# Long convolution of a hybrid layer: folding the forward transform by token parity, adding the bias to the spectrum by DMA, and moving its first half among the hyena projections

## The chip, the cores and the metric

The kernel runs on one core of one Trainium2 chip. The metric is the device time of one execution in microseconds (us), as the median of several executions. TensorE (PE) does the matrix products, VectorE (DVE) and ScalarE (ACT) the elementwise work, GpSimd (POOL) and SyncE (SP) mostly issue DMA transfers.

## What is computed

One layer of a diffusion backbone on 256 latent tokens and 256 context tokens, width 2048, all in float32. A half-step feed-forward block (SwiGLU) comes first and last. Between them one projection feeds two groups of heads: grouped-query attention, and a hyena mixer of width 1024 on the latent tokens. The change is in the mixer:

```
def long_conv(v, kk):                      # v: 256 tokens x 1024 channels, kk: 512 taps
    vf = rfft(v, n=2 * L); kf = rfft(kk, n=2 * L)
    return irfft(vf * kf, n=2 * L)[:L]

def hyena_mixer(u, kk, conv_w, conv_b, hy_bias):
    uc = short_conv(u, conv_w, conv_b)     # three taps
    x0, x1, v = split(uc)
    v = v * x1
    v = long_conv(v, kk) + hy_bias * v
    return v * x0
```

The transform of 256 tokens to 257 frequencies is done as matrix products with cosines and sines, and so is the way back. A term `hy_bias * v` is the same as adding the bias to every value of the real spectrum of the filter.

## The kernel before

**Precision.** Every float32 operand of a product is split in two parts, high and low, in a reduced type that PE takes at full rate: ACT casts the high part, DVE subtracts it from the original to get the low part (`split`, lines 216 to 220; `weight`, lines 237 to 251, for weights that come by DMA as `raw`). `mm3` (lines 253 to 256) then makes three products of each pair: high by high, high by low, low by high (lines 254, 255, 256).

**Order.** The program is written straight down. A planner gives each engine a fixed order when the program is built: among the instructions that its own cost estimates say are ready, the one that stands first in the program. So work of later lines fills gaps when its inputs and its buffers are there. A buffer pool has a fixed number of slots: weights have four `raw` slots, three `whi` and three `wlo` slots; PSUM has four banks `pa` and four `pb`. The DMA transfers of a queue (SP's or POOL's) are issued in that queue's own order.

**Stages around the change**, in the order of time:

1. End of the first feed-forward block's down projection (`Ffn.down`, lines 628 to 659). Its main passes use products of 512 columns; its last two groups (`rest`) are done once for the context tokens and once for the latent tokens, with products of 256 columns, 24 of them for each weight piece of 512 KB (`raw<-in_w_dn`). Between the two kinds stand, in program order, the loads of constants for the mixing stage (`mload`, lines 1068 to 1084): two transform matrices `dftc` and `dfts`, tables for attention and the short convolution, the bias `hyb`, and sixteen loads of the filter's spectrum from DRAM scratch into four tiles `kspec` of 128 frequencies x 1024 channels (real parts in `kspec[0]`, `kspec[1]`, imaginary ones in `kspec[2]`, `kspec[3]`; line 1084, each load 128 rows of 256 channels). All go through SP's queue. The spectrum itself was computed much earlier, beside the first block (`filter_spectrum`); row 0 of its imaginary part carries the 257th frequency.
2. The norms and the key and value projections.
3. The hyena projections: a loop over eight channel tiles `ct` (lines 1232 to 1241). Each takes four weight pieces (`proj_pair`, lines 1219 to 1229: 16 steps of one 512-column and one 256-column product for each of two outputs), then the short convolution `conv` on ACT and DVE (lines 1208 to 1217), which gives the tile `vT[ct]`, and a transpose of a piece of the residual (`turn_x`).
4. The long convolution (lines 1244 to 1294), two halves of 512 channels. A half transposes four `vT` tiles to token-major (lines 1257 to 1262), splits them, multiplies by the cosine and sine matrices (for each of two blocks of 128 frequencies two banks, two token blocks, three products: 12 products of 512 columns a block, 24 a half), multiplies by the filter's spectrum on DVE (lines 1272 to 1281, with three one-row corrections for the packed row 0), splits the result, multiplies back (48 products of 256 columns a half, lines 1286 to 1292) and adds bias times `vT` on DVE while it leaves PSUM (line 1293). Between the blocks the loop advances the first query projection by `QSTEP` weight pieces, so that PE has other work while DVE is busy.
5. The second query projection, the gate projections `x0`, attention (lines 1297 to 1359) and the output projection.

Of the kernel before, what the change touches and what calls it, by code (L numbers as in the profile page):

```python
# [15 lines left out]
ALU = mybir.AluOpType  # L16
# [27 lines left out]

AWAKE = (17, 5)

QSTEP = (2, 1, 3, 2)
FILL = (2, 0)

AWAKE2 = 8  # L50
# [19 lines left out]
def hybrid_layer_kernel(ctx: ExitStack, tc: tile.TileContext, a):  # L70
# [14 lines left out]
    def U(shape, dt=F32):  # L85
        return T(up, shape, "u", dt, 58)

    def tmp(shape):
        return T(up, shape, "sq", bufs=2)
# [7 lines left out]
    def PB(shape=(P, 512)):  # L97
        return T(pp, shape, "pb")
# [117 lines left out]
    def split(src, shape):  # L216
        hi, lo = U(shape, F32R), U(shape, F32R)
        S.copy(hi, src)
        V.tensor_sub(lo, src, hi.bitcast(F32))
        return hi, lo  # L220
# [847 lines left out]
    def mload(name, shape, src=None):  # L1068
        t = T(mp, shape, name)
        nc.sync.dma_start(t, a[name] if src is None else src)  # L1070
        return t

    dftc = mload("dftc", (P, 2, L))
    dfts = mload("dfts", (P, 2, L))
    rope = mload("rope", (P, 2, 2, 64))
    qkg = mload("qkg", (P, 2, P), a["qkg"].partition_broadcast(P))
    convw = mload("convw", (P, 3, 3 * CT))
    convb = mload("convb", (P, 3 * CT))
    hyb = mload("hyb", (P, CT))
    gout = mload("gout", (P, 2 * CT))  # L1080
    kspec = [T(mp, (P, HW), f"kspec{s}") for s in range(4)]
    for n, t in enumerate(spec):
        for f in range(2):
            nc.sync.dma_start(kspec[2 * (n % 2) + f][:, (n // 2) * L : (n // 2 + 1) * L], t[:, f, :])

    f1.hook = lambda: None
    next(more)
# [141 lines left out]
                yield  # L1229

    vT = [U((P, 2, L)) for _ in range(CT // 2)]
    for ct in range(CT):
        pvx = []
        for _ in proj_pair(a["w_hy"][ct], pvx):
            pass
        yv = conv(pvx[0], 2 * CT + ct)
        y1 = conv(pvx[1], CT + ct)
        V.tensor_mul(vT[ct // 2][:, ct % 2, :], yv, y1)
        turn_x(ct % 2, ct // 2)
        if ct == 4:  # L1240
            turn_gates()


    hyT = [U((P, 2, L)) for _ in range(CT // 2)]
    fwd = [split(m, (P, 2, L)) for m in (dftc, dfts)]
    inv = []
    for name in ("idfc", "idfs"):
        m = tmp((P, 2, L))
        nc.sync.dma_start(m, a[name])
        inv.append(split(m, (P, 2, L)))  # L1250
    pq0 = []
    query = proj_steps(a["w_q"][0], [0, 1], pq0)
    next(query)
    for half in range(2):
        hs = slice(half * 512, half * 512 + 512)
        vt = []
        for t in range(2):
            pt = PB((P, 4, P))
            for i in range(4):
                ct = half * 4 + i  # L1260
                PE.transpose(pt[:, i, :], vT[ct // 2][:, ct % 2, t * P : (t + 1) * P], ident)
            vt.append(split(pt.rearrange("p a b -> p (a b)"), (P, 512)))
        yre, yim = [], []
        for f in range(2):
            pr_, pi_ = PB(), PB()
            for ps, mat in ((pr_, fwd[0]), (pi_, fwd[1])):
                for t in range(2):
                    mm3(ps, [m[:, t, f * P : (f + 1) * P] for m in mat], vt[t], t == 0, t == 1)
            kr, ki = kspec[f][:, hs], kspec[2 + f][:, hs]
            a1, a2 = U((P, 512)), U((P, 512))  # L1270
            b1, b2 = U((P, 512)), U((P, 512))
            V.tensor_mul(a1, pr_, kr)
            V.tensor_mul(a2, pi_, ki)
            V.tensor_mul(b1, pr_, ki)
            V.tensor_mul(b2, pi_, kr)
            if f == 0:
                V.tensor_copy(b2[0:1, :], a2[0:1, :])
                V.memset(a2[0:1, :], 0.0)
                V.memset(b1[0:1, :], 0.0)
            V.tensor_sub(a1, a1, a2)  # L1280
            V.tensor_add(b1, b1, b2)
            yre.append(split(a1, (P, 512)))
            yim.append(split(b1, (P, 512)))
            for _ in range(QSTEP[2 * half + f]):
                next(query, None)
        for i in range(4):
            ct = half * 4 + i
            ps = PB((P, L))
            sl = slice(i * P, (i + 1) * P)
            for n, (y_, mat) in enumerate(((yre, inv[0]), (yim, inv[1]))):  # L1290
                for f in range(2):
                    mm3(ps, [m[:, sl] for m in y_[f]], [m[:, f, :] for m in mat], n + f == 0, n + f == 2)
            V.scalar_tensor_tensor(hyT[ct // 2][:, ct % 2, :], vT[ct // 2][:, ct % 2, :], hyb[:, ct : ct + 1], ps,
                                   op0=ALU.mult, op1=ALU.add)


    def gate_steps():
# [541 lines left out]
def _constants():  # L1839
    f32 = np.float32  # L1840
    rows = L // 64
    row = np.repeat(np.arange(rows), 64).astype(f32)
    col = np.tile(np.arange(64), rows).astype(f32)
    inv = (f32(10000.0) ** (-np.arange(0, 64, 2, dtype=f32) / f32(64))).astype(f32)
    ang = np.concatenate([row[:, None] * inv, col[:, None] * inv], axis=-1).astype(f32)
    rope = np.stack([np.cos(ang.astype(np.float64)), np.sin(ang.astype(np.float64))], axis=1).astype(f32)
    rope = rope.reshape(2, P, 2, 64).transpose(1, 0, 2, 3)

    t = np.linspace(0.0, 1.0, L, dtype=f32)[:, None]
    w = (f32(2.0 * math.pi) * np.arange(L, dtype=f32)[:, None] / f32(L)).astype(f32)  # L1850
    f = np.linspace(1e-4, 15, 16, dtype=f32)[None, :]
    fw = (f * w).astype(f32).astype(np.float64)
    z = np.concatenate([t, np.cos(fw).astype(f32), -np.sin(fw).astype(f32)], axis=-1).astype(f32)

    eo = np.r_[0:L:2, 1:L:2]
    z = z[eo]
    tneg = np.stack([*(-t[:, 0])[eo].reshape(2, P), 1.0 - 2.0 * (np.arange(P) % 2)], axis=1).astype(f32)

    n = np.arange(L)
    th = 2.0 * np.pi * np.outer(n, n) / (2 * L)  # L1860
    alt = (1.0 - 2.0 * (n % 2))
    cos_, sin_ = np.cos(th), np.sin(th)

    fdft = np.stack([m[eo, :P].reshape(2, P, P) for m in (cos_, sin_)])
    fdft[1, 1, :, 0] = 1.0 - 2.0 * (np.arange(P) % 2)
    fdft = fdft.transpose(2, 0, 1, 3).astype(f32)

    fr = np.r_[0 : P + 1, L - 1 : P : -1]

    def tp(m):  # L1870
        return np.ascontiguousarray(m.reshape(2, P, -1).transpose(1, 0, 2)).astype(f32)

    sinv = sin_.copy()
    sinv[:, 0] = alt
    wt = np.full((L, 1), 2.0)
    wt[0] = 1.0
    ic = cos_ * wt / (2 * L)
    isn = sin_ * 2.0 / (2 * L)
    isn[0] = alt / (2 * L)
    return dict(rope=np.ascontiguousarray(rope), zT=np.ascontiguousarray(z.T), tneg=tneg,  # L1880
                fdft=np.ascontiguousarray(fdft), dftc=tp(cos_[:, fr]), dfts=tp(sinv[:, fr]), idfc=tp(ic[fr]), idfs=tp(isn[fr]))


def _prepare(i):
# [51 lines left out]
    d["qkg"] = np.stack([eo(i["q_norm"][0]), eo(i["k_norm"][0])])  # L1936
    d["convw"] = c_(i["conv_w"][0].reshape(3, 3 * CT, P).transpose(2, 0, 1))
    d["convb"] = pcol(i["conv_b"][0])
    d["hyb"] = pcol(i["hy_bias"][0])
    d["gout"] = pcol(i["g_out"][0])  # L1940
    w1, w2, w3, d["flt_w4"] = (c_(i[f"flt_w{n}"][0]) for n in (1, 2, 3, 4))
    head = np.zeros((P, 4, 64), np.float32)
# [24 lines left out]
```

## Time and profile before

| | |
|---|---|
| median of three timed executions | 2575.5 us (2574.84 to 2576.6) |
| the profiled execution's own time | 2573.66 us |
| its span | 2571.9 us, 38718 instructions |
| mean granted PE clock | 0.998 |
| busy share PE / DVE / ACT / POOL | 99% / 84% / 47% / 14% |
| hyena projections and long convolution | about 1531 to 1677 us of the span |
| loads of the mixing constants | 1422.7 to 1434.5 us of the span |

A line of the timeline has the start in us from the span's start, the duration, engine, line of the program, operation, output<-inputs, shape, and how many are merged into it; in brackets the idle time before it and what ended that. `PEld` is a weight load, `SPq` a DMA issue of SP. A line of the windows has the stretch, its length, then the busy time and the number of instructions of each engine, the granted clock, the mean busy share of the 16 DMA engines, and GB/s.

### The profile page before, as it was taken

How to read it: one execution, taken by the hardware profiler on the slowest of the kernel's cores; microseconds unless marked ns; L12 is line 12 of the kernel's file. 1: busy time of each engine (PE TensorE's matmuls, PEld its weight loads, DVE VectorE, ACT ScalarE, POOL GpSimd, SP SyncE). 2: the span in 40 equal slices, each digit the busy share in tenths (PEclk: the TensorE clock that was granted, in tenths of full speed). 3: DMA queues.
4: the chain of work that ended last, by engine and by line, in shares of the span. 5: the costliest groups of instructions: out<-in, count | busy, mean ns of one | idle time of the engine just before them, and what ended most of it. 6: DMA issues, size and time to landing. Idle time of an engine off the chain costs nothing.

```text
span 2571.9 us, 38718 instructions
## 1 busy us (share of the span) xinstructions
PE 2555.1 (99%) x14333; PEld 2198.3 (85%) x14333; DVE 2164.1 (84%) x3498; ACT 1213.6 (47%) x1702; POOL 365.1 (14%) x587
## 2 busy tenths in 40 slices
PE   8999999999999999999999999999999999999999
PEld 5678999999999999888888988888888888888887
DVE  6876888888888896777989796789789999999998
ACT  5454444444444443111211455457466666665554
POOL 1132222222222223320010000000000001012010
PEclk9999999999999999999999999999999999999999
DMA  9997889888888899996798556335757878789784
GB/s 364 383 290 209 250 243 254 242 243 248 253 247 255 243 252 317 395 363 209 260 328 287 178 167 194 123 123 162 232 172 237 246 240 265 236 265 310 236 286 159
DMA packets 209387, 640.77 MB, mean 249 GB/s; under 512 B 24715, under 2 KB 27756, under 8 KB 204844
## 3 DMA queue, kind: packets, MB, share of 16 engines
q1 hardware_dynamic: 134396, 482.37, 55.6%
q0 software_dynamic: 74608, 155.78, 23.4%
q8 instruction: 112, 1.84, 0.3%
q14 instruction: 79, 0.65, 0.1%
q10 hardware_dynamic: 192, 0.13, 0.0%
HBM read 558.73 MB, written 48.53 MB: 236 GB/s over the span
## 4 chain that ended last, share of the span: by engine, by line
PE 97%; DMA 1%; DVE 1%; ACT 0%; issue 0%; SPq 0%; ACTq 0%; DVEq 0%
PE pb L254 10%; PE pb L255 10%; PE pb L256 10%; PE pa L254 9%; PE pa L255 9%; PE pa L256 9%; PE pa L1394 6%; PE pa L1395 6%; PE pa L1396 6%; PE pb L1394 4%; PE pb L1396 4%; PE pb L1395 4%; PE pa L262 3%; PE pa L264 2%; PE pa L1110 1%; PE pa L1111 1%
## 5 line engine op out<-in xcount | busy, mean ns | idle before, releaser
L243 ACT CAST whi<-raw 128x1024 fp32r<-128x1024 f32 x235 | 247.2, 1052 | 500.4 <-PE pb L255 192.3
L247 DVE TENSOR_TENSOR wlo<-raw,whi 128x1024 fp32r<-128x1024 f32 x235 | 286.9, 1221 | 134.5 <-ACT whi L243 133.5
L254 PE MATMUL pa<-u,whi 128*128 128x256 f32 (+1 forms) x912 | 306.6, 337 | 2.1 <-ACT u L907 2.1
L255 PE MATMUL pa<-u,whi 128*128 128x256 f32 (+1 forms) x912 | 304.8, 334 | 0.9 <-DVE u L912 0.9
L256 PE MATMUL pa<-u,wlo 128*128 128x256 f32 (+1 forms) x912 | 304.5, 334 | 0.0
L254 PE MATMUL pb<-u,whi 128*128 128x256 f32 (+1 forms) x904 | 300.1, 332 | 0.0
L255 PE MATMUL pb<-u,whi 128*128 128x256 f32 (+1 forms) x904 | 298.4, 330 | 0.0
L256 PE MATMUL pb<-u,wlo 128*128 128x256 f32 (+1 forms) x904 | 298.3, 330 | 0.0
L466 ACT CAST bhi<-raw 128x768 fp32r<-128x768 f32 x111 | 92.5, 833 | 265.1 <-PE pb L255 131.1
L158 DVE CUSTOM_DVE_ANT_0 adas<-adaw,crow,cond 128x1024 bf16<-128x1024 f32 x160 | 205.0, 1281 | 14.5 <-DMA adaw<-in_w_adaT_dram 12.7
L158 DVE CUSTOM_DVE_ANT_0 adas<-adaw,crow,mod 128x1024 bf16<-128x1024 f32 x160 | 205.0, 1281 | 13.3 <-DMA adaw<-in_w_adaT_dram 11.3
L254 PEld LDWEIGHTS pa<-u,whi 128*128 128x128 f32 x912 | 172.9, 190 | 24.6 <-issue 4.5
L255 PEld LDWEIGHTS pa<-u,whi 128*128 128x128 f32 x912 | 173.5, 190 | 17.7 <-DVE u L912 1.7
L256 PEld LDWEIGHTS pa<-u,wlo 128*128 128x128 f32 x912 | 173.5, 190 | 17.2
L254 PEld LDWEIGHTS pb<-u,whi 128*128 128x128 f32 x904 | 171.8, 190 | 17.4 <-issue 2.0
L469 DVE TENSOR_TENSOR blo<-raw,bhi 128x768 fp32r<-128x768 f32 x111 | 106.3, 957 | 94.1 <-ACT bhi L466 94.1
L255 PEld LDWEIGHTS pb<-u,whi 128*128 128x128 f32 x904 | 171.9, 190 | 15.7 <-issue 0.4
L256 PEld LDWEIGHTS pb<-u,wlo 128*128 128x128 f32 x904 | 171.8, 190 | 15.6
L1396 PE MATMUL pa<-whi,u 128*128 128x512 f32 x451 | 175.8, 390 | 0.0
L1394 PE MATMUL pa<-whi,u 128*128 128x512 f32 x450 | 175.7, 391 | 0.0
L1395 PE MATMUL pa<-wlo,u 128*128 128x512 f32 x450 | 175.6, 390 | 0.1
L277 ACT CAST whi<-raw 128x1024 fp32r<-128x1024 f32 x122 | 126.9, 1052 | 98.4 <-DVE raw L277 63.0
(476 smaller groups left out, 6689.8 us busy)
## 6 DMA issues: line engine op xcount, KB each, us to landing
adaw<-in_w_adaT_dram SPq DMA_DIRECT2D x224, 512.0 KB, 5.8
raw<-in_w_up1q_dram SPq DMA_DIRECT2D x124, 512.0 KB, 5.2
raw<-in_w_up2p_dram SPq DMA_DIRECT2D x107, 512.0 KB, 4.7
raw<-in_w_dn_dram SPq DMA_DIRECT2D x94, 512.0 KB, 6.0
u<-act POOLq DMA_DIRECT2D x172, 256.0 KB, 9.6
wrow<-in_w_ada_dram SPq DMA_DIRECT2D x32, 1024.0 KB, 10.1
raw<-in_w_dn2p_dram SPq DMA_DIRECT2D x59, 512.0 KB, 5.3
vraw<-in_w_up2p_dram SPq DMA_DIRECT2D x53, 512.0 KB, 4.8
```

The costliest lines, as they stand in the source:

```text
L158: V.tensor_tensor_reduce(out=sc, in0=t, in1=crow[i][:, b * (D // 2) : (b + 1) * (D // 2)], scale=1.0, scalar=mcol if b else bada[:, c * KT ...
L243: last_hi[0] = S.copy(hi, raw)
L247: last_lo[0] = V.tensor_sub(lo, raw, hi.bitcast(F32))
L254: PE.matmul(ps, w[0], xx[0], start=start, stop=False)
L255: PE.matmul(ps, w[0], xx[1], start=False, stop=False)
L256: return PE.matmul(ps, w[1], xx[0], start=False, stop=stop)
L277: return do(*args, **kw)
L466: return raw, hi, lo, S.copy(hi, raw[:, :, 0:3])
L469: return V.tensor_sub(lo, raw[:, :, 0:3], hi.bitcast(F32))
L1394: PE.matmul(ps[t], hi, w[0], start=start, stop=False)
L1395: PE.matmul(ps[t], hi, w[1], start=False, stop=False)
L1396: last = PE.matmul(ps[t], lo, w[0], start=False, stop=stop)
```

## The change

- **Matrices.** `dftc` and `dfts` (256 tokens x 256 frequencies each) give way to one tile `dftf` of four 128 x 128 blocks: cosine and sine, for even and for odd tokens, at the first 128 frequencies. It is split at `ct == 2` of the hyena loop; the matrices of the way back are loaded and split at `ct == 4` and `ct == 5`.
- **Forward transform.** The transposes now take every second token (`t::2`). For cosine and for sine, one bank gets the product with the even tokens, another that with the odd ones: 12 products of 512 columns for a half instead of 24. ACT copies the odd bank to SBUF; DVE's sum of even and odd gives one block of frequencies, their difference the other, mirrored block. Three one-row copies on ACT repair the packed row.
- **Spectrum product.** The four products per block read SBUF instead of PSUM. The three one-row corrections on DVE are gone; instead row 0 of `kspec[2]` is set to zero, and after the first product with it ACT overwrites row 0 of `kspec[0]` with the row `last_row`.
- **Bias.** The product with `hyb` is gone; PSUM is copied out by ACT. Instead `kspec[0]` and `kspec[1]` get the bias added by two accumulating DMAs of POOL's queue (128 rows of 1024 values, the bias row repeated), and `last_row` by two small ones.
- **Loads.** SP's burst loses `dftc`, `dfts` and `hyb` and gains `dftf`, and four loads of one row each into `last_row`. Of the sixteen `kspec` loads, the four that fill `kspec[2]` leave row 0 out: `r0` is 1 there, so they have rows 1 to 127.
- **Order.** `long_steps(half)` is a generator with seven yields. Half 0 is advanced at each of the three yields of `proj_pair` from `ct == 4` on; half 1 runs after the loop, with `QSTEP` query pieces after each of its yields.

```diff
-QSTEP = (2, 1, 3, 2)
+QSTEP = (1, 1, 1, 1, 2, 1, 1)
...
-    dftc = mload("dftc", (P, 2, L))
-    dfts = mload("dfts", (P, 2, L))
+    dftf = mload("dftf", (P, 4, P))
...
-    hyb = mload("hyb", (P, CT))
...
     for n, t in enumerate(spec):
         for f in range(2):
-            nc.sync.dma_start(kspec[2 * (n % 2) + f][:, (n // 2) * L : (n // 2 + 1) * L], t[:, f, :])
+            r0 = (n % 2) * (1 - f)
+            nc.sync.dma_start(kspec[2 * (n % 2) + f][r0:P, (n // 2) * L : (n // 2 + 1) * L], t[r0:P, f, :])
+    last_row = U((P, 512))
+    for n in range(4):
+        nc.sync.dma_start(last_row[32 * (n // 2) : 32 * (n // 2) + 1, (n % 2) * L : (n % 2 + 1) * L], spec[2 * n + 1][0:1, 0, :])
+    G.memset(kspec[2][0:1, :], 0.0)
+    for t in kspec[0:2]:
+        nc.gpsimd.dma_start(t, a["hyb"].partition_broadcast(P), accum_op=ALU.add)
+    for n in range(2):
+        nc.gpsimd.dma_start(last_row[32 * n : 32 * n + 1, :], a["hyb"][:, n * 512 : (n + 1) * 512], accum_op=ALU.add)
...
+    def long_steps(half):
+        hs = slice(half * 512, half * 512 + 512)
+        vt, yre, yim, parts = [], [], [], []
+        for t in range(2):
+            pt = PB((P, 4, P))
+            for i in range(4):
+                ct = half * 4 + i
+                PE.transpose(pt[:, i, :], vT[ct // 2][:, ct % 2, t::2], ident)
+            vt.append(split(pt.rearrange("p a b -> p (a b)"), (P, 512)))
+        yield
+        for sn in range(2):
+            pe, po, odd = PB(), PB(), U((P, 512))
+            for ps, t in ((po, 1), (pe, 0)):
+                mm3(ps, [m[:, 2 * sn + t, :] for m in fwd], vt[t], True, True)
+            S.copy(odd, po)
+            parts.append((U((P, 512)), U((P, 512))))
+            V.tensor_add(parts[sn][0], pe, odd)
+            V.tensor_sub(parts[sn][1], *((odd, pe) if sn else (pe, odd)))
+            if not sn:
+                yield
+        (_, c1), (s0, s1) = parts
+        S.copy(s0[0:1, :], c1[0:1, :])
+        S.copy(c1[0:1, :], pe[0:1, :])
+        S.copy(s1[0:1, :], odd[0:1, :])
+        yield
+        for f in range(2):
+            kr, ki = kspec[f][:, hs], kspec[2 + f][:, hs]
+            a1, b2 = parts[0][f], parts[1][f]
+            a2, b1 = U((P, 512)), U((P, 512))
+            V.tensor_mul(b1, a1, ki)
+            V.tensor_mul(a1, a1, kr)
+            if f == 0:
+                S.copy(kr[0:1, :], last_row[32 * half : 32 * half + 1, :])
+            V.tensor_mul(a2, b2, ki)
+            V.tensor_mul(b2, b2, kr)
+            V.tensor_sub(a1, a1, a2)
+            V.tensor_add(b1, b1, b2)
+            yre.append(split(a1, (P, 512)))
+            yim.append(split(b1, (P, 512)))
+            yield
+        for cp in range(2):
+            hyT[2 * half + cp] = U((P, 2, L))
+            for i in range(2):
+                ps = PB((P, L))
+                sl = slice((2 * cp + i) * P, (2 * cp + i + 1) * P)
+                for n, (y_, mat) in enumerate(((yre, inv[0]), (yim, inv[1]))):
+                    for f in range(2):
+                        mm3(ps, [m[:, sl] for m in y_[f]], [m[:, f, :] for m in mat], n + f == 0, n + f == 2)
+                S.copy(hyT[2 * half + cp][:, i, :], ps)
+            yield
...
     for ct in range(CT):
+        if ct == 2:
+            fwd = next(made)
+        if ct in (4, 5):
+            inv = inv + [next(made)] if ct == 5 else [next(made)]
+        if ct == CT // 2:
+            part = long_steps(0)
         pvx = []
         for _ in proj_pair(a["w_hy"][ct], pvx):
-            pass
+            if ct >= CT // 2:
+                next(part, None)
...
+    for _ in part:
+        pass
     next(query)
...
+    for n, _ in enumerate(long_steps(1)):
+        for _ in range(QSTEP[n]):
+            next(query, None)
```

On the host, `dftf` replaces `dftc` and `dfts`, and `hyb` becomes one row of 1024 values.

More of the change, by code (lines that the diff above doesn't have):

```diff
@@ L1231, in hybrid_layer_kernel, with matrices @@
     vT = [U((P, 2, L)) for _ in range(CT // 2)]
-    for ct in range(CT):
+    hyT = [None] * (CT // 2)
+    def matrices():
+        yield split(dftf, (P, 4, P))
+        for name in ("idfc", "idfs"):
+            m = tmp((P, 2, L))
+            nc.sync.dma_start(m, a[name])
+            yield split(m, (P, 2, L))
+    def long_steps(half):
[48 more added lines that the diff above has]
+            yield
@@ L1233, in hybrid_layer_kernel @@
+    pq0 = []
+    query = proj_steps(a["w_q"][0], [0, 1], pq0)
+    made = matrices()
+    for ct in range(CT):
+        if ct == 2:
[4 more added lines that the diff above has]
+            part = long_steps(0)
         pvx = []
         for _ in proj_pair(a["w_hy"][ct], pvx):
-            pass
+            if ct >= CT // 2:
+                next(part, None)
         yv = conv(pvx[0], 2 * CT + ct)
@@ L1241, in hybrid_layer_kernel @@
             turn_gates()
[L1244 to L1252, printed above, removed]
-    next(query)
[L1254 to L1294, printed above, removed]
@@ L1865, in _constants @@
     fdft[1, 1, :, 0] = 1.0 - 2.0 * (np.arange(P) % 2)
-    fdft = fdft.transpose(2, 0, 1, 3).astype(f32)
+    dftf = fdft.copy()
+    dftf[1, 0, :, 0] = 1.0 - 2.0 * (np.arange(P) % 2)
+    dftf, fdft = (np.ascontiguousarray(m.transpose(2, 0, 1, 3)).astype(f32) for m in (dftf, fdft))
+    dftf = dftf.reshape(P, 4, P)
     fr = np.r_[0 : P + 1, L - 1 : P : -1]
@@ L1871, in tp @@
         return np.ascontiguousarray(m.reshape(2, P, -1).transpose(1, 0, 2)).astype(f32)
-    sinv = sin_.copy()
-    sinv[:, 0] = alt
     wt = np.full((L, 1), 2.0)
@@ L1880, in _constants @@
     return dict(rope=np.ascontiguousarray(rope), zT=np.ascontiguousarray(z.T), tneg=tneg,
-                fdft=np.ascontiguousarray(fdft), dftc=tp(cos_[:, fr]), dfts=tp(sinv[:, fr]), idfc=tp(ic[fr]), idfs=tp(isn[fr]))
+                fdft=np.ascontiguousarray(fdft), dftf=dftf, idfc=tp(ic[fr]), idfs=tp(isn[fr]))
 def _prepare(i):
@@ L1938, in _prepare @@
     d["convb"] = pcol(i["conv_b"][0])
-    d["hyb"] = pcol(i["hy_bias"][0])
+    d["hyb"] = c_(i["hy_bias"][0].reshape(1, HW))
     d["gout"] = pcol(i["g_out"][0])
```

## The prediction

> **What bounds the kernel now.** The busy times first, then the chain of waits.
>
> ```profile
> PE 2555.1 (99%) x14333; PEld 2198.3 (85%) x14333; DVE 2164.1 (84%) x3498; ACT 1213.6 (47%) x1702; POOL 365.1 (14%) x587
> ...
> PE 97%; DMA 1%; DVE 1%; ACT 0%; issue 0%; SPq 0%; ACTq 0%; DVEq 0%
> ```
>
> PE is the bound nearly everywhere: a product taken away is worth its full time, and a wait put in front of PE costs its full time. The windows show how much room the other engines have in the hyena loop (first row) and in the long convolution (the others).
>
> ```profile
> 1580.00:1600.00 20.00, 20.00 (x118) 17.50 (x117) 12.94 (x20) 10.82 (x16) 0.00 (x0) 1.00 0.65 202
> ...
> 1625.00:1677.00 52.00, 51.94 (x291) 44.98 (x290) 45.27 (x78) 22.12 (x35) 0.00 (x0) 1.00 0.32 102
> ```
>
> In the loop DVE is busy 65% and ACT 54%; in the long convolution DVE is at 87%, and PE still runs through. "Busy" is not peak, so I take PE's price from starts, in the timeline of PE:
>
> ```profile
> 1635.30 0.39 PE L255 MATMUL pb<-u,u 128*128 128x512 f32 x1
> ...
> 1640.28 0.39 PE L1111 MATMUL pa<-whi,u 128*128 128x512 f32 x1
> ```
>
> Between these two starts lie 22 products of 512 columns: 4.98 / 22 = 0.226 us each.
>
> **Part 1, the products removed.** 12 fewer products of 512 columns in each half, 24 x 0.226 = **-5.4 us**. The 48 products back and the eight transposes of a half stay. The transposes read every second token; eight take 0.79 us (1655.28 to 1656.07 below). No row has such a stride: none or double gives 0 to +1.6 us for both halves; I take 0, since the row nearest is the same transpose without it.
>
> ```profile
> 1655.28 1.03 PE L1261 MATMUL pb<-ident,u 128*128 128x128 f32 x8
> 1656.07 0.47 PE L1109 MATMUL pa<-whi,u 128*128 128x512 f32 x1
> ```
>
> **Part 2, DVE and ACT.** Starts of consecutive 128x512 operations on DVE lie 0.60 us apart:
>
> ```profile
> 1637.27 0.68 DVE L1272 TENSOR_TENSOR u<-pb,kspec 128x512 f32<-128x512 f32 x1
> 1637.87 0.68 DVE L1273 TENSOR_TENSOR u<-pb,kspec 128x512 f32<-128x512 f32 x1
> ...
> 1639.79 0.48 DVE L1279 MEMSET u<- 1x512 f32 x1
> 1640.21 0.35 DVE L1277 COPY u<-u 1x512 f32<-1x512 f32 x1
> ...
> 1641.13 0.62 DVE L1281 TENSOR_TENSOR u<-u,u 128x512 f32<-128x512 f32 x1
> ...
> 1654.04 1.27 DVE L1293 SCALAR_TENSOR_TENSOR u<-u,hyb,pb 128x256 f32<-128x256 f32 x3 [0.70 <-PE pb L256]
> ...
> 1613.16 0.77 ACT L1211 COPY sg<-pa 128x256 f32<-128x256 f32 x2 [1.55 <-PE pa L262]
> ...
> 1627.32 0.57 ACT L1124 COPY u<-pb 128x512 f32<-128x512 f32 x1
> ```
>
> A half gains four sums and differences (+2.4 us) and loses three one-row operations (-1.3, from 1639.79 to 1641.13) and four bias operations (1.27 / 3 = 0.42 each, -1.7): DVE is even. With 22 operations of 0.6 us (8 products, 8 sums and differences, 6 low parts) that is 13 us a half. ACT gains two copies of 128x512 (0.57), four of 128x256 (0.39) and four of one row (no such row on ACT: between DVE's 0.35 and a full copy's 0.57), 4 to 5 us a half; at 43 to 54% busy it has room.
>
> Half 0 now lies among the projections of ct 4 to 6.
>
> ```profile
> 1601.57 0.60 PE L1122 MATMUL pb<-ident,u 128*128 128x128 f32 x4
> ...
> 1613.32 0.60 PE L1122 MATMUL pb<-ident,u 128*128 128x128 f32 x4
> ...
> 1652.40 0.28 PE L254 MATMUL pb<-u,u 128*128 128x256 f32 x1
> ...
> 1653.60 0.28 PE L255 MATMUL pb<-u,u 128*128 128x256 f32 x1
> ```
>
> A ct lasts 11.75 us (from one transpose of `turn_x` to the next), a product of 256 columns 1.20 / 10 = 0.12. So PE has 3 x 11.75 us and 9.3 us of half 0 (12 x 0.226 + 48 x 0.12 + 0.8), 44.6 us; DVE has 0.65 x 35.3 = 22.9, the half's 13 and 1.8 for the matrices' low parts, 37.7 us: 85%, no more than the 87% at which it did not hold PE up before. I take 0. The other end: the product steps of ct 5 (9.6 us), the four sums (2.4), one convolution (2.5) and four low parts of weights (4.6) make 18.5 us of DVE within one ct of 11.75 us, 6.8 too many; the weight buffers give one piece of lead, 2.9 us, so up to +3.9.
>
> Half 1 has all eight query pieces (8 x 12 x 0.226 = 21.7 us of PE) as its cover instead of four. What it may win back is the one hole of this stretch:
>
> ```profile
> 1677.32 0.28 PE L264 MATMUL pa<-u,wlo 128*128 128x256 f32 x1
> 1678.77 0.47 PE L1109 MATMUL pa<-whi,u 128*128 128x512 f32 x1 [1.17 <-DVE small L291]
> ```
>
> PE starts the second query projection 1.3 us late, for a bank that DVE frees behind the second half's work. Afterwards the query ends last and its norm has only two pieces of gate projections (5.9 us) as cover, but an emptier DVE. Between 0 and -1.3: **-0.5 us**.
>
> **Part 3, the loads.** The burst of constants stands in front of the weights of the down projection's last groups, in SP's queue:
>
> ```profile
> 1422.73 0.33 SPq L1070 DMA_DIRECT2D dftc<-in_dftc_dram  x1
> ...
> 1426.42 8.06 SPq L1084 DMA_DIRECT2D kspec<-spec  x16
> 1434.58 19.47 SPq L231 DMA_DIRECT2D raw<-in_w_dn_dram  x11
> ```
>
> 24 issues take 11.85 us, 0.49 each; the changed burst has 26 (+1.0 us). What follows is tight. ACT's timeline, then DVE's and PE's:
>
> ```profile
> 1435.64 1.05 ACT L243 CAST whi<-raw 128x1024 fp32r<-128x1024 f32 x1 [4.38 <-PE pb L255]
> 1440.78 1.05 ACT L243 CAST whi<-raw 128x1024 fp32r<-128x1024 f32 x1 [4.09 <-DMA raw<-in_w_dn_dram]
> ...
> 1441.87 2.53 DVE L247 TENSOR_TENSOR wlo<-raw,whi 128x1024 fp32r<-128x1024 f32 x2 [3.92 <-ACT whi L243]
> ...
> 1441.42 0.28 PE L254 MATMUL pa<-u,whi 128*128 128x256 f32 x1
> ...
> 1444.30 0.28 PE L254 MATMUL pa<-u,whi 128*128 128x256 f32 x1
> 1444.54 0.28 PE L256 MATMUL pa<-u,wlo 128*128 128x256 f32 x1
> ```
>
> A piece lasts PE 2.88 us. The cast at 1435.64 serves the piece at 1441.42; the next cast waits for its DMA until 1440.7, its low part ends at 1443.1, and PE uses it from 1444.54. The lead is **1.4 us**; whatever delays this `raw` further, PE waits for. Behind PE's wait stand the rest of the down projection, the residual, the norms, the key projection: nothing else can fill it.
>
> Now the four `kspec[2]` loads of 127 rows. No load of 127 rows is in the trace. The two ends: as cheap as those of 128 rows, or all rows through one of the 16 DMA engines.
>
> ```profile
> kspec<-spec SPq DMA_DIRECT2D x16, 128.0 KB, 2.9
> ...
> rope<-in_rope_dram SPq DMA_DIRECT2D x1, 128.0 KB
> ...
> convb<-in_convb_dram SPq DMA_DIRECT2D x1, 12.0 KB, 3.8
> ...
> mt<-in_zT_dram SPq DMA_DIRECT2D x1, 33.0 KB
> ```
>
> The nearest row is `zT`, the one load of a row count (33) that 16 doesn't divide. It has no landing time, nor has `rope`, which shares its semaphore: counted in the trace, that semaphore got 1868 counts for 117 DMAs, the seven others of that queue 1872, which is 16 a DMA. For `zT` itself there are 12: one at once, then eleven. Eleven engines of three rows explain that; 127 has no divisor up to 16 but 1. So I take **one engine**.
>
> The Trainium skill ("DMA: Bandwidth & Descriptors", section "Why a DMA increments its semaphore by 16 and not by 1") says just this: the largest number up to 16 that divides the rows, 127 rows on one engine, and the issuer writes the missing counts at once. The trace agrees in `zT`'s 12; by the page the load is not spread, and the sum is the one below.
>
> The price: in the burst all engines move 251 GB/s at 83%, in the next row 303 at 93%; a sixteenth at full share is 18.9 to 20.4 GB/s.
>
> ```profile
> 1428.00:1434.00 6.00, 6.00 (x28) 4.99 (x27) 4.36 (x11) 1.06 (x1) 0.00 (x0) 1.00 0.83 251
> ...
> 1434.50:1441.00 6.50, 6.50 (x51) 6.27 (x50) 2.08 (x3) 1.27 (x2) 0.00 (x0) 1.00 0.93 303
> ...
> 1953.50:1961.00 7.50, 7.50 (x35) 6.21 (x34) 7.43 (x14) 5.55 (x9) 1.17 (x2) 1.00 1.00 231
> ...
> wlo<-raw POOLq DMA_DIRECT2D x8, 512.0 KB, 5.6
> ```
>
> 127 rows of 1 KB take 6.4 to 6.9 us, four 25.5 to 27.5. The first is the ninth issue, at 1426.5, its data some 2.5 us later (2.9 to landing less 0.4 of data). The same engine has its sixteenth of ten other `kspec` loads (80 KB, 4.0 to 4.3 us) and of the first `raw` (32 KB, 1.6 to 1.7), behind them in its queue. That `raw` lands at 1429.0 + 31.1 to 33.5 = 1460.1 to 1462.5 instead of 1440.7. The bias DMAs come on top: `kspec[0]` is complete behind three long loads, at 1429.0 + 3 x 6.4 to 6.9 + 4, near 1453; two transfers of 512 KB, as accumulating ones run (231 GB/s), put 64 KB at 14.4 GB/s, 4.5 us, on that engine. So 1460.1 to 1467.0, in the middle 1463.5; less 1440.7 and the lead of 1.4, PE waits 18 to 25 us, **+21**. The next three `raw` are queued right behind and land 1.7 us apart, against 2.88 of PE: no second wait.
>
> **Sum.** -5.4 - 0.5 + 21 = +15.1 us on the profiled execution's 2573.66, 2588.8. The runs' median lies 1.8 above that execution: **2590.5**. A change under 0.2% (5.2 us) cannot be told from none here.
>
> **Rivals.** *Spread after all* (not slower): the 127 rows go to all engines. Then the first `raw` is late by 1.0 us of issue and by up to 4.5 us of bias traffic, if both 512 KB get in front (DMA share 93% there speaks for it), less the lead: 0 to 4, say 2 us; 2575.5 - 5.9 + 2 = 2571.6. Point of decision: whether the first `raw` lands by 1442. `zT` speaks against. Chance 14%, half of it faster than the bound. *Weights ahead*: the planner lets the three `raw` past the burst; then PE waits three pieces later, 8.6 us less: 2582. That SP issued all 24 first before speaks against; 8%. *Crowded loop*: the wait and DVE's 3.9 us in ct 4 to 6: 2594.4; the stretch at 87% speaks against; 5%.
>
> **How the numbers follow.** One engine: 73%, with its own range 2584 to 2600 (waits of 18 to 25, one engine alone perhaps quicker than one of sixteen, the loop's and the transposes' bounds above). With weights ahead and crowded loop, 2578 to 2600 holds 8 in 10. Slower: 73 + 5 + 5 of the 8; the same: 7 + 3; faster: 7.
>
> **What would show it.** PE idle for about 20 us in the down projection's last groups, ended by a `raw` that lands over 20 us after its issue, with a low DMA share meanwhile, proves part 3; a `raw` landing in 7 us refutes it. 24 fewer products at 0.226 apart show part 1. The bank wait before the second query projection and DVE's share in ct 4 to 6 show part 2.

## Result: 2590.9 us against 2575.8 us, 0.6% slower

The changed kernel takes 2590.9 us (median of 6 executions, 2590.32 to 2591.44); the kernel before, run beside it, 2575.78 us (2574.59 to 2576.6). The ratio is 1.0059, with a 95% interval of 1.0048 to 1.0069. The profiled execution took 2590.87 us, with a span of 2589.1 us.

The busy times and the chain of waits, after:

```profile
PE 2555.3 (99%) x14309; PEld 2196.3 (85%) x14309; DVE 2161.7 (83%) x3491; ACT 1221.9 (47%) x1721; POOL 368.4 (14%) x592
...
PE 95%; DMA 2%; DVE 1%; SPq 1%; ACT 1%; issue 0%; ACTq 0%; DVEq 0%
```

PE has the 24 fewer instructions (14309 for 14333). The part of the span in which it is idle grew from 16.8 to 33.8 us (2571.9 less 2555.1, 2589.1 less 2555.3), and the chain has two points more outside PE. The list of PE's waits after (who waited for whom: us in all, how many, the longest) names one wait that is larger than all others together:

```profile
PE pa L254 <- ACT whi L243: 17.5, 1, 17.5
PE pb L197 <- DMA wrow<-in_w_ada_dram: 2.2, 3, 1.3
...
PE pa L1425 <- DVE wlo L247: 0.7, 1, 0.7
...
PE pa L1116 <- DVE u L1157: 0.3, 1, 0.3
```

It stands in the down projection's last groups. The timelines of ACT and of PE there, after:

```profile
1435.80 1.05 ACT L243 CAST whi<-raw 128x1024 fp32r<-128x1024 f32 x1 [4.38 <-PE pb L255]
1461.02 1.04 ACT L243 CAST whi<-raw 128x1024 fp32r<-128x1024 f32 x1 [24.17 <-DMA raw<-in_w_dn_dram]
...
1444.34 0.28 PE L256 MATMUL pa<-u,wlo 128*128 128x256 f32 x1
1462.12 0.58 PE L254 MATMUL pa<-u,whi 128*128 128x256 f32 x1 [17.50 <-ACT whi L243]
1462.50 0.41 PE L255 MATMUL pa<-u,whi 128*128 128x256 f32 x1
1463.38 0.58 PE L256 MATMUL pa<-u,wlo 128*128 128x256 f32 x1 [0.46 <-DVE wlo L247]
```

The cast that waited for its weights until 1440.78 before now waits until 1461.02. Why the weights came so late is seen in the timeline of SP's queue, the first lines of it over the whole burst, then three narrow windows of it, then in POOL's queue:

```profile
1425.16 0.43 SPq L1070 DMA_DIRECT2D gout<-in_gout_dram  x1
1425.64 22.71 SPq L1083 DMA_DIRECT2D kspec<-spec  x16
1448.44 26.30 SPq L231 DMA_DIRECT2D raw<-in_w_dn_dram  x11
...
1429.87 5.23 SPq L1083 DMA_DIRECT2D kspec<-spec  x1
...
1436.59 5.31 SPq L1083 DMA_DIRECT2D kspec<-spec  x1
...
1443.23 5.12 SPq L1083 DMA_DIRECT2D kspec<-spec  x1
...
1448.62 1.82 POOL L1089 DMA_DIRECT2D kspec<-in_hyb_dram  x2 [24.75 <-DMA kspec<-spec]
```

The sixteen `kspec` issues took 8.06 us before and take 22.71 us now. Three of them last 5.1 to 5.3 us instead of about 0.5, which is 14.2 of the 14.65 us. Each of the three is a load of 128 rows that stands directly behind the second, third or fourth load of 127 rows. So SP itself was held, and the first of the late `raw` loads was not issued until 1448.44 (before: 1434.58), 13.9 us later. It then needed 12.6 us to its cast (before: 6.2). The traffic of all 16 DMA engines shows both stages, in slices of 1.125 us from 1420 to 1465 (GB/s) and in the windows (DMA share and GB/s are the last two numbers, the granted PE clock the one ahead of them), after:

```profile
GB/s 15 0 0 62 335 119 232 34 225 142 25 24 24 25 243 131 24 23 24 24 233 142 23 24 24 51 189 311 368 276 250 261 287 261 274 288 146 29 25 87
```

```profile
1440.00:1445.00 5.00, 4.62 (x39) 4.41 (x37) 0.00 (x0) 0.00 (x0) 0.00 (x0) 1.00 0.31 97
1445.00:1450.00 5.00, 0.00 (x0) 0.00 (x0) 0.00 (x0) 0.00 (x0) 1.38 (x2) 0.69 0.28 60
1450.00:1455.00 5.00, 0.00 (x0) 0.00 (x0) 0.00 (x0) 0.00 (x0) 0.44 (x1) 0.50 0.97 287
1455.00:1460.00 5.00, 0.00 (x0) 0.00 (x0) 0.00 (x0) 0.00 (x0) 0.00 (x0) 0.50 1.06 274
...
1462.00:1467.50 5.50, 4.92 (x21) 4.62 (x22) 3.74 (x4) 2.25 (x4) 0.00 (x0) 0.51 0.52 156
1467.50:1471.00 3.50, 3.50 (x32) 3.50 (x30) 2.18 (x3) 3.04 (x4) 0.00 (x0) 1.00 0.65 225
```

Three times the rate falls to 23 to 25 GB/s for three or four slices. 127 KB at 24 GB/s are 5.4 us, as long as SP's holds. Then, from 1450, all engines are full: the delayed weights and the two bias transfers of 512 KB, which POOL issued at 1448.6 when their spectrum loads had landed, go at the same time. The rows of the fourth short load move beside them.

What the 12.6 us between issue and cast were is told by the semaphore counts of the trace, the same kind of count as the prediction made for `zT`. Each load of 127 rows has two, one at its issue and one at its end; the four ends are at 1434.2, 1440.8, 1447.4 and 1457.4 us. The first `raw` has sixteen: fifteen come from 1452.0 to 1452.7, the last at 1460.9, just ahead of ACT's cast. So fifteen of its sixteen shares were there 8.2 us earlier, and PE waited for the share that stood behind the fourth short load on the one engine.

The same windows show a loss that the idle time doesn't hold: PE goes on at a clock of 0.5 from 1462.12 to about 1467.4, 5.3 us, of which 0.46 are the second wait; half of the other 4.8, about 2.4 us, is lost. 17.50 + 0.46 + 2.4 = 20.4 us. The start of the hyena loop (first row of each pair) is later by 20.7 (0.16 of that stands ahead of the wait: the cast at 1435.80 was at 1435.64 before), and the first products behind the second query projection (second row) by 15.0. PE's timelines, first before, then after:

```profile
1530.99 0.60 PE L1204 MATMUL pb<-ident,u 128*128 128x128 f32 x4
...
1682.27 0.38 PE L1354 MATMUL pb<-ident,u 128*128 128x128 f32 x2
```

```profile
1551.71 0.60 PE L1211 MATMUL pb<-ident,u 128*128 128x128 f32 x4
...
1697.31 0.60 PE L1384 MATMUL pb<-ident,u 128*128 128x128 f32 x4
```

So the stretch that holds the fold and the new order became 5.7 us shorter (151.28 to 145.60), and the burst of loads cost nearly four times that (5.7 against 20.7). Of the 17.2 us between the two spans the last 2.2 come later; 0.7 of them is the wait for `wlo` at L1425 in the list above, and the rest I did not place. The medians differ by 15.1.

### The profile page after: what moved, and what is told of

The parts are those of the page before. It is cut to its first block, busy times and chain, and to the rows that moved or that the text cites. A ratio compares the mean times of both kernels' runs of the same rounds, so it can differ in the third digit from the quotient of the medians.

```text
span 2589.1 us, 38713 instructions
## 1 busy us (share of the span) xinstructions
PE 2555.3 (99%) x14309; PEld 2196.3 (85%) x14309; DVE 2161.7 (83%) x3491; ACT 1221.9 (47%) x1721; POOL 368.4 (14%) x592
## 4 chain that ended last, share of the span: by engine, by line
PE 95%; DMA 2%; DVE 1%; SPq 1%; ACT 1%; issue 0%; ACTq 0%; DVEq 0%
PE pb L254 9%; PE pb L255 9%; PE pb L256 9%; PE pa L254 9%; PE pa L255 9%; PE pa L256 9%; PE pa L1424 6%; PE pa L1425 6%; PE pa L1426 6%; PE pb L1424 4%; PE pb L1425 4%; PE pb L1426 4%; PE pa L262 3%; PE pa L264 2%; PE pa L1117 1%; PE pb L197 1%
## 5 line engine op out<-in xcount | busy, mean ns | idle before, releaser
L254 PE MATMUL pa<-u,whi 128*128 128x256 f32 (+1 forms) x912 | 307.7, 338 | 19.6 <-ACT whi L243 17.5
L158 DVE CUSTOM_DVE_ANT_0 adas<-adaw,crow,cond 128x1024 bf16<-128x1024 f32 x160 | 205.1, 1282 | 17.2 <-DMA adaw<-in_w_adaT_dram 15.5
L254 PEld LDWEIGHTS pa<-u,whi 128*128 128x128 f32 x912 | 173.9, 191 | 42.4 <-ACT whi L243 17.7
L1425 PE MATMUL pa<-wlo,u 128*128 128x512 f32 x450 | 175.7, 390 | 0.9 <-DVE wlo L247 0.7
```

What stands on the lines that cost most here:

```text
L158: V.tensor_tensor_reduce(out=sc, in0=t, in1=crow[i][:, b * (D // 2) : (b + 1) * (D // 2)], scale=1.0, scalar=mcol if b else bada[:, c * KT ...
L254: PE.matmul(ps, w[0], xx[0], start=start, stop=False)
L1425: PE.matmul(ps[t], hi, w[1], start=False, stop=False)
```

## Experiments

The theory after the result: four loads of 127 rows run on one engine and hold SP, the weights behind them are issued late and their last share waits on that engine, and the fold itself gives its products back. Its rivals: the delay comes from the larger burst or from the bias transfers; the clock takes the larger part; the fold or the new place is worth nothing. A ratio is to the kernel before, run on the same chip; 0.001 is 2.6 us.

### The rows alone

*All rows* (label full_rows): the changed kernel, with 128 rows in all sixteen loads.

```diff
-            r0 = (n % 2) * (1 - f)
+            r0 = 0
```

> The changed kernel with all sixteen spectrum loads at 128 rows (row 0 of kspec[2] is zeroed behind them). One-engine theory (a load of 127 rows runs on one DMA engine and SP's queue is held until it drains): the burst ends near 1433 us instead of 1448, the wait of 17.7 us in the down projection falls to 0 to 3 us (what the bias DMAs still cost, which now start near 1436), and the time is 2575.8 - 5.7 + 0 to 3 = 2570 to 2573 us. Bias theory (the accumulating bias DMAs at 97 to 106% DMA share hold the weights back, the 127 rows are innocent): the wait stays and the time is 2586 to 2591.

*126 rows* (rows_126): the four short loads cut into row 1 and rows 2 to 127, so that row 0 still isn't loaded.

```diff
+            cut = (slice(1, 2), slice(2, P)) if n % 2 > f else (slice(0, P),)
+            for r in cut:
+                nc.sync.dma_start(kspec[2 * (n % 2) + f][r, ...], t[r, f, :])
```

> The changed kernel with each short load cut in two: row 1 alone and rows 2 to 127, 126 rows, which 14 divides. One-engine theory, with the engines dealt by a divisor of the row count: 14 engines, no held queue, 2571 to 2574 us (four more issues, 2 us of burst). If any load that does not begin at row 0, or whose row count 16 does not divide, is slow: four slow loads as before, 2588 to 2592. Bias theory: 2586 to 2591.

*Two of four* (two_short): only the first two of the four loads have 127 rows.

```diff
-            r0 = (n % 2) * (1 - f)
+            r0 = (n % 2) * (1 - f) * (n < 4)
```

> The changed kernel with 127 rows in two of the four kspec[2] loads and 128 in the other two. One-engine theory: two loads hold SP for some 10 us less than four do, the wait is 7 to 11 us instead of 17.7, and the time about 2579 to 2584. Bias theory: 2586 to 2591, as with four.

*The kernel before, with short loads* (before_short): nothing of the change but the rows; the same four loads are cut into row 0 and rows 1 to 127.

```diff
+            cut = (slice(0, 1), slice(1, P)) if n % 2 > f else (slice(0, P),)
+            for r in cut:
+                nc.sync.dma_start(kspec[2 * (n % 2) + f][r, ...], t[r, f, :])
```

> The kernel before with nothing changed but the four kspec[2] loads: row 0 in a load of its own, rows 1 to 127 in another. No bias DMAs, no fold. One-engine theory: SP is held as in the changed kernel, the first weights are issued near 1450 us and land 6 us later, PE waits 12 to 16 us and runs at a lower clock after it: 2588 to 2593 us. Bias theory: no change but 2 us of issue, 2575 to 2578.

| kernel | median us | ratio, 95% interval | SP's `kspec` issues, us |
|---|---|---|---|
| changed | 2590.9 | 1.0059 (1.0048 to 1.0069) | 22.71 for 16 |
| all rows | 2575.56 | 0.9995 (0.9987 to 1.0004) | 7.93 for 16 |
| 126 rows | 2572.87 | 0.9987 (0.9978 to 0.9997) | 8.23 for 20 |
| two of four | 2582.73 | 1.0028 (1.0018 to 1.0039) | 15.84 for 16 |
| before, short loads | 2594.91 | 1.0072 (1.0058 to 1.0086) | 23.66 for 20 |

SP's timeline with all rows, then SP's, ACT's and PE's in the kernel before with short loads, then the DMA rates of the latter (1420 to 1465, as above):

```profile
1428.30 7.93 SPq L1082 DMA_DIRECT2D kspec<-spec  x16
1436.32 23.19 SPq L231 DMA_DIRECT2D raw<-in_w_dn_dram  x11
```

```profile
1430.48 23.66 SPq L1086 DMA_DIRECT2D kspec<-spec  x20
1454.24 1.91 SPq L231 DMA_DIRECT2D raw<-in_w_dn_dram  x4
...
1462.64 1.04 ACT L243 CAST whi<-raw 128x1024 fp32r<-128x1024 f32 x1 [21.89 <-DMA raw<-in_w_dn_dram]
...
1463.74 0.58 PE L254 MATMUL pa<-u,whi 128*128 128x256 f32 x1 [15.23 <-ACT whi L243]
```

```profile
GB/s 0 153 313 0 15 0 20 290 322 125 123 117 131 141 126 24 23 23 36 251 108 24 23 23 23 221 152 23 23 23 28 215 356 356 331 328 363 51 25 25
```

One row more in four loads takes all of the loss away, one row less (126) does so too, and half of the short loads cost about half. In the kernel before, without any other part of the change, the short loads cost 18.5 us and show the same three plateaus. It is the count of rows and not the bytes, the fold, the bias transfers (the kernel before has none), or the larger burst: with 126 rows the burst has more issues than the changed one and is not held. The semaphore counts agree: a load of 126 rows has fifteen, one at its issue and fourteen behind, where one of 127 has two. All slow loads begin at row 1; one of 127 rows that begins at row 0 was not run.

The kernel before with short loads also tells the engine's backlog from the bias traffic. Its first `raw` needs 8.4 us from issue to cast (1454.24 to 1462.64): fifteen of its counts are there by 1458.3, the last comes at 1462.5, behind the end of the fourth short load at 1461.1. That is 2.2 us more than the 6.2 of the kernel before, and the changed kernel's 12.6 are 4.2 more still, which is about what the bias transfers add. With two short loads SP takes 7.9 us more than with none: 4.8 come from one held issue (5.3 where others take 0.43), and 2.8 are a gap in which SP waits to use the second short load's semaphore again (the queue's eight are used in turn), which is free when that load lands, at 1441.3.

### Whose queue

*Short loads from GpSimd* (pool_127): the rows as changed; only who issues the four loads differs.

```diff
...
+            queue = nc.gpsimd if r0 else nc.sync
-            nc.sync.dma_start(kspec[...][r0:P, ...], t[r0:P, f, :])
+            queue.dma_start(kspec[...][r0:P, ...], t[r0:P, f, :])
```

> The changed kernel with its four loads of 127 rows issued by GpSimd instead of by SyncE; rows and placing unchanged, the loads of 128 rows stay on SyncE. The raw loads of the down projection are then issued some 21 us earlier than in the changed kernel if what delayed them was SyncE's own issue, held for 5.3 us per load of 127 rows: 2571 to 2579, with GpSimd held instead and the bias loads landing later. If the delay is in the transfer engine that the loads of 127 rows share, whoever issues them (the prediction's account), the raw loads still wait behind them there: 2587 to 2592.

2574.28 us, ratio 0.9997 (0.9988 to 1.0007). This kernel's timelines of SP's and of POOL's queue, then its DMA issues (the last number is the landing time), then its window over them:

```profile
1426.16 6.17 SPq L1084 DMA_DIRECT2D kspec<-spec  x12
1432.42 25.62 SPq L231 DMA_DIRECT2D raw<-in_w_dn_dram  x11
...
1423.68 2.19 POOL L1084 DMA_DIRECT2D kspec<-spec  x4 [40.62 <-DVE mod L158]
```

```profile
kspec<-spec POOLq DMA_DIRECT2D x4, 127.0 KB, 4.1
```

```profile
1425.00:1430.00 5.00, 5.00 (x23) 4.13 (x22) 3.84 (x10) 1.06 (x1) 1.78 (x3) 1.00 0.91 286
```

The time is that of the first way, but its reason isn't the one I gave: POOL isn't held (2.19 us for four issues), and the loads land in 4.1 us while 286 GB/s flow. From this queue 127 rows are spread, so the run has neither the hold nor the single engine and can't tell one from the other. That SP is held stands on its own timeline alone, and that PE in the end waited for the one engine on the semaphore counts above. The Trainium skill ("DMA: Bandwidth & Descriptors", section "Why a DMA increments its semaphore by 16 and not by 1") has this exception beside the rule that the prediction used: some direct copies whose descriptors GpSimd makes are spread by rows rounded up per engine, 127 over all sixteen. The run agrees with it, by its 4.1 us against the 5.4 that one load takes on one engine at 24 GB/s, and 21 that four would take there.

### The bias transfers and the place of the loads

*Bias later* (bias_late): all rows, and the bias transfers held until the down projection is done.

```diff
...
+    gate = G.tensor_copy(T(mp, (P, 1), "gate"), xd(0, KT - 1)[:, L - 1 : L])
+    with tc.issue_after(gate.ins):
+        for t in kspec[0:2]:
+            nc.gpsimd.dma_start(t, a["hyb"].partition_broadcast(P), accum_op=ALU.add)
...
```

> The kernel of full_rows (all spectrum loads at 128 rows) with the bias DMAs held until the down projection is done. In full_rows PE still waited 1.4 + 0.9 us in the down projection, with the first weights landing 9 us after their issue while the bias DMAs ran. If the bias traffic is that remainder, the weights land in 6 to 7 us again, no wait is left there, and the time falls by 2 to 3 us against full_rows: about 0.998 of the kernel before (-4 to -6 us). If it is the burst itself, the wait of 2 to 3 us stays: 0.9985 to 1.0.

*All loads later* (late_all): the spectrum loads (all rows), `last_row` and the bias stand behind the down projection's last weights.

```diff
     for _ in downs:
         pass
+    with tc.issue_after(loads[-1].ins):
+        for n, t in enumerate(spec):
+            for f in range(2):
+                nc.sync.dma_start(kspec[2 * (n % 2) + f][:, ...], t[:, f, :])
+    ...
```

> The changed kernel with the sixteen spectrum loads (128 rows) and the four one-row loads behind the down projection's last weights, and the bias DMAs behind them. No burst but six constants stands in front of the weights. If only the order of transfers hid the gain of the fold: 24 products x 0.226 = 5.4 us and no wait left, 0.9975 to 0.998 (-5 to -6.5 us). If the fold's gain is lost in the hyena loop as well (DVE crowded in ct 4 to 6): 0.999 to 1.0.

Bias later: 2571.06 us, 0.9985 (0.9976 to 0.9994). All loads later: 2570.9 us, **0.9983 (0.9974 to 0.9992)**, faster than the kernel before and than the changed one. In both the wait in the down projection is gone. With all rows and the bias early it was 1.3 and 0.8 us, from the list of PE's waits of that kernel; the timeline of SP's queue with all loads later follows:

```profile
PE pa L254 <- ACT whi L243: 1.3, 1, 1.3
...
PE pa L256 <- DVE wlo L247: 0.8, 1, 0.8
```

```profile
1426.31 27.27 SPq L231 DMA_DIRECT2D raw<-in_w_dn_dram  x11
1453.63 9.02 SPq L1091 DMA_DIRECT2D kspec<-spec  x16
```

The bias transfers alone, early, thus cost about 0.001, 2.6 us, in two runs whose intervals overlap; the 2.1 us of wait that go with them speak for the same. All rows is what the prediction's rival *Spread after all* would have been. Its 2 us for this wait hold, but its 2571.6 does not: 2575.56 came out, and by the ratio 2.6 us of its gain are missing. They are not lost in the fold: the stretch from the start of the hyena loop to behind the second query projection is 145.55 us here too (1537.73 to 1683.28). The trace of this kernel has PE's clock at 0.76 from 60 to 67 us and at 0.83 from 1495 to 1505, 1.7 us lost each time; the kernel with 126 rows has 1.00 in both windows and came to 0.9987, near the rival's figure. That these steps of the clock are the missing time in all executions is not shown.

### The fold and the new place

*Unfolded* (late_unfolded): all loads later, with the forward transform as before, 24 products of 512 columns more, copied out by ACT.

```diff
...
-            for ps, t in ((po, 1), (pe, 0)):
-                mm3(ps, [m[:, 2 * sn + t, :] for m in fwd], vt[t], True, True)
+                for t in range(2):
+                    mm3(ps, [m[:, t, f * P : (f + 1) * P] for m in fwd[sn]], vt[t], t == 0, t == 1)
...
```

> late_all with the forward transform unfolded again: 24 more products of 128 x 512 (8 groups of 6 instead of 8 groups of 3), four ACT copies per half in place of the even and odd sums; placement and bias loads as in late_all (0.9983 of before). If the fold is worth its products on TensorE, as the prediction has it (24 x 0.226 = 5.4 us): 0.9983 + 0.0021 = 1.0004, about 2576. If the products that the fold takes away had been hidden behind waits anyway, the time is that of late_all, 2571.

2575.84 us, 1.0002 (0.9993 to 1.0011). Against all loads later that is 0.0019, 4.9 us, for products priced at 5.4; the two intervals leave about 1.5 to 8 us. PE's timelines are sharper. With all loads later, then unfolded, the stretch from the start of the hyena loop to behind the second query projection is 145.59 and 151.07 us, 5.5 apart:

```profile
1533.13 0.60 PE L1212 MATMUL pb<-ident,u 128*128 128x128 f32 x4
...
1678.72 0.60 PE L1385 MATMUL pb<-ident,u 128*128 128x128 f32 x4
```

```profile
1533.22 0.60 PE L1213 MATMUL pb<-ident,u 128*128 128x128 f32 x4
...
1684.29 0.60 PE L1381 MATMUL pb<-ident,u 128*128 128x128 f32 x4
```

The fold is worth its products, and without it nothing of the gain is left: place and bias together are worth zero, to within 2 or 3 us by the interval.

*Both halves behind the loop* (late_no_move): all loads later, the fold stays, no half among the projections; four query pieces beside each half.

```diff
-            if ct >= CT // 2:
-                next(part, None)
+            pass
...
-QSTEP = (1, 1, 1, 1, 2, 1, 1)
+QSTEP = (1, 1, 0, 1, 1, 0, 0)
```

> late_all with both halves of the long convolution behind the hyena loop, four query pieces of cover each, as before the change. If the place among the projections is worth nothing by itself (the stretch before lost only some 2 to 3 us of PE time in 52): the same as late_all within 1 us. If the place is part of the gain: 2 to 4 us slower than late_all. If the crowded loop costs: 1 to 4 us faster.

*The same with three and five pieces* (late_no_move_35):

```diff
-QSTEP = (1, 1, 0, 1, 1, 0, 0)
+QSTEP = ((0, 1, 1, 1, 0, 0, 0), (1, 1, 1, 1, 1, 0, 0))
```

> late_no_move with its cover split otherwise: of the nine pieces of the second query projection, three go to the first half of the convolution and five to the second, after the one ahead of both (late_no_move: four and four). If the 4.0 us wait in the second half's inverse, which late_no_move showed, came from that split alone, it goes: 2571 to 2572, and the place among the projections is worth nothing, as the prediction has it. If the convolution after the loop lacks cover altogether, the wait stays or moves to the first half: 2574 to 2577, and the place is worth those 4 to 5 us.

With four and four: 2575.74 us, 1.0005 (0.9996 to 1.0014). PE's timeline shows a wait in the second half's way back:

```profile
1673.78 0.39 PE L254 MATMUL pb<-u,u 128*128 128x256 f32 x1 [3.88 <-ACT u L218]
```

With three and five: 2572.22 us, 0.9989 (0.998 to 0.9998), and the wait at the same place is smaller:

```profile
1670.94 0.39 PE L254 MATMUL pb<-u,u 128*128 128x256 f32 x1 [1.58 <-ACT u L218]
```

After the first of the two I had taken the place to be worth nearly 5 us. The second shows that most of it was the split of the cover, one query piece more or less. What is left is 1.3 us between the medians of this one and of all loads later, with intervals that overlap: the place is worth 0 to 2 us or so. The traces say 0.6: the stretch takes 146.23 us here (1531.82 to 1678.05) and 145.59 with all loads later.

### The clock after the wait

*Kept busy* (awake): the changed kernel, with 72 products of ones, 128 columns each (144 instructions in the trace, from 1445.5 to 1461.5 us), in front of the piece that waits, so that PE's clock doesn't fall.

```diff
...
+                        if part and g == rest[0] and dq == PASSES[-1][2]:
+                            bank = PB()
+                            with tc.issue_after(self.last.ins):
+                                for _ in range(72):
+                                    PE.matmul(bank[:, 0:P], ones, ones, start=True, stop=True)
```

> The changed kernel, short loads and all, with 72 products of ones by ones (0.22 us each, some 16 us) put into PE's order in front of the piece that waits. In the changed kernel the granted clock falls to 0.50 in the wait and is back at 1.0 only some 8 us after PE goes on. If that costs what the longer starts after the wait show (about 3 us): the clock stays near 1.0 and the time is 2 to 3 us under the changed kernel's, about 2588 (ratio 1.0047). If the products only fill the wait and the clock doesn't matter: the same as the changed kernel, 1.0055 to 1.006. If they outlast the wait: slower.

2590.84 us, 1.0062 (1.0048 to 1.0075): no difference. The windows of this kernel, then PE's timeline:

```profile
1455.00:1460.00 5.00, 5.00 (x47) 5.00 (x46) 0.00 (x0) 0.00 (x0) 0.00 (x0) 1.00 1.04 263
1460.00:1465.00 5.00, 2.45 (x19) 2.06 (x18) 1.44 (x2) 2.09 (x2) 0.00 (x0) 1.00 0.54 153
1465.00:1470.00 5.00, 5.00 (x31) 5.00 (x31) 3.09 (x5) 2.84 (x5) 0.00 (x0) 0.66 0.76 227
```

```profile
1463.52 0.39 PE L254 MATMUL pa<-u,whi 128*128 128x256 f32 x1 [1.79 <-ACT whi L243]
...
1464.78 0.39 PE L256 MATMUL pa<-u,wlo 128*128 128x256 f32 x1 [0.76 <-DVE wlo L247]
```

The products ended 1.8 us before the high part of the weights was there, and PE waited 0.8 us more for the low part, with two products in between. The clock fell all the same, only later and for a shorter time (0.66 over 5 us, 1.7 us lost in place of 2.4). At most one microsecond was to be won, which these runs can't tell. So the cost of the clock rests on the trace alone, in which 17.50 + 0.46 + 2.4 make up all but 0.3 of the shift of 20.7.

## Why the prediction was right, and where it was wrong

**The sum.** Forecast 2590.5, measured 2590.9. It holds because its large terms hold, not because every step does: within the +21 several sizes were off, and that they cancel to less than 1 us is luck.

**Part 1, the fold: right.** -5.4 forecast. The stretch became 5.7 us shorter with the bank wait's share in it, and the unfolded kernel gives 4.9 by its times and 5.5 by its stretch. The strided transposes at 0 were right: six of them take 0.64 us in PE's timeline after (1602.04 to 1602.68), 0.107 each, where eight took 0.79 before, 0.099 each.

**Part 2, DVE and half 0 in the loop: right.** 85% of DVE was forecast for ct 4 to 6. The window over that stretch, after, has 36.25 / 45 = 81% and PE without a gap, so *Crowded loop* didn't come:

```profile
1598.50:1643.50 45.00, 45.00 (x273) 39.52 (x272) 36.25 (x57) 27.86 (x46) 0.00 (x0) 1.00 0.44 142
```

The wait ahead of the second query projection was to shrink by 0.5 and shrank by 0.9 (1.17 before, 0.3 in the list of PE's waits after). That all eight pieces were needed as cover for half 1 was not said: beside a half behind the loop, four pieces leave a wait of 3.9 us and five one of 1.6. The four terms of the crowded end add up to 19.1 us and not 18.5, so its bound was +4.5 rather than +3.9, and the rival's 2594.4 would be 2595.0; neither came.

**Part 3, +21: the path right, four sizes off.** That 127 rows go through one engine holds: two semaphore counts for a load, and 24 GB/s for as long as a load lasts, three times over. *"Behind them in its queue"* holds as well: the last share of the first `raw` came at 1460.9, 8.2 us after the fifteen others and behind the fourth short load. The next two `raw` followed 1.3 us apart (their last counts are at 1462.2 and 1463.5), so there was no second wait. What the prediction didn't have is that SP itself is held: it had the first `raw` issued on time, and in the trace it was issued 13.9 us late, when only the fourth short load was still ahead of it. What the hold costs by itself no run shows; the engine had the same rows to move ahead of `raw` either way. The sizes:

- *The price per load* was too high: 5.1 to 5.3 us where 6.4 to 6.9 stood, 4 to 7 us for the four. The forecast had taken a sixteenth of the rate that all engines had together while they were busy, 18.9 to 20.4 GB/s; this engine moved 24 while the others stood idle.
- *The bias on top* was priced at 0 to 4.5 us on that engine, with the middle of the range used. About 4.2 are measured, as the difference between two kernels that differ in more (12.6 and 8.4 us from issue to cast), so it lies at the upper end. ACT's cast at 1461.0 is inside 1460.1 to 1467.0 because this error and that of the price per load have opposite signs.
- *The lead of 1.4* is that of the low part. The first product needs only the high part, which had 2.5 us: 20.2 us late (1461.02 less 1440.78) leaves 17.7 of wait, 17.5 was measured, and 0.46 follows for the low part. The wait is thus just under the forecast's 18 to 25.
- *The clock* was left out, and filled the gap: about 2.4 us lost at half speed behind the wait. The Trainium skill ("TensorE: Matmul & The Clock Gate", section "Part 1: The HAM clock gate (the "warmup" mystery)") says that an idle PE drops to half its clock after a window of about 3.4 us and needs a busy one to come back. On the way back the trace agrees: 5.3 us from the first product until the clock was 1.00, more than one such window and less than two. The fall came sooner than a full window of idle time: 0.69 over 1445 to 1450 puts it at 1446.9, 2.3 us behind the last product.

**The burst of 26 (+1.0 us): wrong.** It has 22 issues. The planner put the four loads of `last_row` 50 us earlier, as the answer on their line shows (count, shortest, median and longest ns, first and last start):

```profile
L1086 SPq DMA_DIRECT2D u<-spec x4: 263/284/364, 1371.4 to 1375.8; - x4
```

*Weights ahead*, in which the weights overtake the burst, didn't come: SP's line above has all sixteen loads first. It is what the kernel with all loads later does by hand.

## What to carry to other kernels

Cutting one row off a DMA can cost more than the row ever did: look at what its row count does to the spread over engines, and at what stands behind it in the issuing queue and on the one engine, since that is what waits. A saving in a dense stretch of PE is worth its products, but loads that stand ahead of urgent weights can hide it. When PE is made to wait, add the slow clock after the wait to the bill.

## What the runs showed of the hardware that was not expected

- Loads that lie on one engine held the queue that issued them. Behind the second to fourth load of 127 rows the next issue took 5.1 to 5.3 us instead of about 0.5, as long as that engine needs for 127 KB at 24 GB/s. Behind the first load there was no such hold. That the one engine's list has room for little more than one such load would fit; no run shows its size.
- A transfer that is spread over all engines is late with a single one of them: fifteen shares of the first `raw` were there by 1452.7, the sixteenth at 1460.9.
- The same 127 rows from GpSimd's queue were spread and held nobody: 2.19 us for four issues, 4.1 us to landing.
- Two accumulating transfers of 512 KB beside the weights filled all engines (share 0.97 and 1.06) for 10 us; started early, they cost about 2.6 us in the kernel with all rows (the difference of two ratios whose intervals overlap).
- Less than 3 us of idle time was enough for a step at half clock: 1.8 and 0.8 us with two products in between in the kernel kept busy, and 2.3 us until the clock fell in the changed one.
